# A decoder step on one core: the three gathered blocks taken through selection first, the short sequences placed beside the other five

## The chip, the core and the metric

The kernel runs on one core of a Trainium2 chip. A core has five engines that work side by side, each with its own queue in the order of the program: PE (TensorE, matmuls; PEld is its loading of weights), DVE (VectorE), ACT (ScalarE), POOL (GpSimd) and SP (SyncE). They meet by semaphores. DMAs are issued from the queues of SP, ACT and POOL. The metric is the device time of one execution in microseconds (us); lower is better.

## What is computed

One layer for 1024 prompt tokens (8 blocks of 128) and for 8 short sequences of 4 new tokens each, which attend to 2048 cached positions in pages. The reference, cut to what matters:

```python
def _layer(x, pos, h0, attend, ...):
    xn = _rmsnorm(x, norm_mix)
    z = xn @ w_in
...
    o_lat = attend(q_nope, q_rope, c_kv, k_rope, w_uk, g_kn)
    o_att = jnp.einsum('bthc,chd->bthd', o_lat, w_uv)
    y_ssm, h_last = _s5(u, h0, a_re, a_im, log_dt, b, c, d_skip)
    gl = jax.nn.gelu(y_ssm) @ w_glu
    glu = gl[..., :SSM_WIDTH] * jax.nn.sigmoid(gl[..., SSM_WIDTH:])
    x = x + jnp.concatenate([glu, o_att], axis=-1) @ w_out
    x = x + _peer(_rmsnorm(x, norm_ffn), peer_wq, peer_keys, peer_u, peer_v)

def block(xb):
    q = (xb @ wq).reshape(PEER_BLOCK, PEER_HEADS, 2, PEER_HALF)
    s = jnp.einsum('qhcd,ckd->qhck', q, keys)
    s1, i1 = lax.top_k(s[:, :, 0], PEER_TOPK)
    s2, i2 = lax.top_k(s[:, :, 1], PEER_TOPK)
    cand = (s1[..., :, None] + s2[..., None, :]).reshape(PEER_BLOCK, PEER_HEADS, kk)
    cidx = (i1[..., :, None] * PEER_KEYS + i2[..., None, :]).reshape(PEER_BLOCK, PEER_HEADS, kk)
    top, sel = lax.top_k(cand, PEER_TOPK)
    idx = jnp.take_along_axis(cidx, sel, axis=-1)
    g = jax.nn.softmax(top, axis=-1)
    act = jax.nn.gelu(jnp.einsum('qhkd,qd->qhk', jnp.take(u_tab, idx, axis=0), xb))
    return jnp.einsum('qhk,qhkd->qd', g * act, jnp.take(v_tab, idx, axis=0))
```

`attend` is causal over the prompt, and for the short sequences it goes over the cache and the new tokens. `block` is the inside of `_peer` for 128 tokens: it finds 128 of 16384 experts for each token (8 heads, 16 each) by scores against two sets of 128 keys, the best 16 of each and the best 16 of their sums, then takes a dot product with the expert's row of `peer_u` and a weighted sum of its rows of `peer_v`.

## The kernel before

The order of each engine's queue is made at build time: the Python code emits instructions in program order, a scheduler with a model of durations moves ready ones up, and tiles that share memory wait for each other. The stages, from `build`:

- Input projection, S5 and the preparation of queries and keys, to about 367 us.
- `attention` for all 8 blocks, one unit a head and block: `scores` writes `s` on PE (one buffer), DVE takes the maximum `mx`, ACT the exponent `p`, `weigh` turns `p` on PE into `pt`, DVE and ACT copy it to `pT`, PE adds `po`. `close` ends a block. The job passed to it, `split_wq`, splits the query weights of PEER into two parts and writes them to `wq_d`.
- `mix_out` for all blocks: the output projection `oz` with `w_out`, the residual and the norm; rows go to `x1_d` and `xn_d` in DRAM.
- `score` for all blocks in 16 steps (`m`): a weight tile `rw` from `wq_d` on POOL's queue, `rq` (24 matmuls a chunk), `rsc` against the keys, and `top16` on DVE for each block.
- `select`: the second top 16 and the turning of places into expert numbers, nearly all on DVE (`cand`, `top`, `sel`, `ri`, `rj`, `eq`, `kn`).

The 8 prompt blocks then go two ways. The first three (`early`, `D0 = 3`) are *gathered* by `Sparse`: for each of 128 places a row of `peer_u` and later of `peer_v` per token is fetched by an indirect DMA on POOL's queue into a ring of five rows (`RB`), and DVE does a dot product (`pu`, `pact`) or a multiply-add (`pacc`). With the short sequences that makes 832 gather steps. The other five (`late`) are *dense*: `Gates` writes a table of gates for all experts to `g_d` (`gps` on PE, `h` and `hv` on DVE), and `Dense` multiplies all of `peer_u` and `peer_v` (`da`, `dres`, `dy`), in 32 groups of four.

`Sample` is the attention of the short sequences: per sequence a `cache` gather on POOL, transposes `ltp`, splits `slh` and `sll`, products `kk`, sums of squares `ssq` on DVE, then `soften` (with the scores `sno`) and `gather`. Its `run` yields after each of 8 steps a sequence. In the code before it stands after the selection of the late blocks, but its memory is set aside early, and the scheduler moves its steps up, to beside attention.

`weave` runs `rest` (what follows the first selection) and `sparse.run` together: each yielded weight, times `PACE` 0.3, lets out gather steps of 1.5, and `behind` holds their issue behind the last DVE and PE instruction so far. In the dense stage the weight is 5.7 times `DENSE_PACE`.

## Time and profile before

| | us |
|---|---|
| median of 3 runs | 3618.16 (3617.83 to 3625.24) |
| the profiled execution | 3620.32, its span 3617.9 |
| PE busy | 3347.4 (93%) |
| DVE busy | 2716.4 (75%) |
| POOL busy | 1233.4 (34%) |
| ACT busy | 1156.2 (32%) |

A busy PE is one with a matmul in flight; two neighbours overlap, so sums of durations are above busy time, and a stretch's busy time is what counts. The granted clock is 1.0 at 2.4 GHz and 0.5 at 1.2 GHz; a value between is a mean over the stretch. Stages with different limits follow each other, so shares of the whole span say little: the rows below are by stage.

### The profile page before, as it was taken

How to read it: one execution, taken by the hardware profiler on the slowest of the kernel's cores; microseconds unless marked ns; L12 is line 12 of the kernel's file. 1: busy time of each engine (PE TensorE's matmuls, PEld its weight loads, DVE VectorE, ACT ScalarE, POOL GpSimd, SP SyncE). 2: the span in 40 equal slices, each digit the busy share in tenths (PEclk: the TensorE clock that was granted, in tenths of full speed). 3: DMA queues.
4: the chain of work that ended last, by engine and by line, in shares of the span. 5: the costliest groups of instructions: out<-in, count | busy, mean ns of one | idle time of the engine just before them, and what ended most of it. 6: DMA issues, size and time to landing. Idle time of an engine off the chain costs nothing.

```text
span 3617.9 us, 52406 instructions
## 1 busy us (share of the span) xinstructions
PE 3347.4 (93%) x19464; PEld 2929.9 (81%) x19464; DVE 2716.4 (75%) x5777; ACT 1156.2 (32%) x2268; POOL 1233.4 (34%) x1044
## 2 busy tenths in 40 slices
PE   8899899999999634998799999999999999999999
PEld 7778687765799523987798898889988989998898
DVE  7674664434577998779688888888888888888884
ACT  4333454422322422456522121222222222222221
POOL 1020100000000104222155556555555556555551
PEclk9889799999999866778899999999999999999999
DMA  3335931143322207777899999999999999999992
GB/s 132 86 88 155 315 130 46 48 152 111 115 82 71 87 26 250 290 248 252 294 308 312 318 318 325 320 315 341 321 314 313 342 333 318 326 317 324 327 328 104
DMA packets 324606, 832.19 MB, mean 230 GB/s; under 512 B 36696, under 2 KB 150488, under 8 KB 313536
## 3 DMA queue, kind: packets, MB, share of 16 engines
q0 software_dynamic: 130608, 510.98, 39.9%
q1 hardware_dynamic: 92752, 247.75, 20.0%
q10 hardware_dynamic: 100992, 70.13, 6.7%
q8 instruction: 153, 2.51, 0.3%
q14 instruction: 101, 0.83, 0.1%
HBM read 734.44 MB, written 92.94 MB: 229 GB/s over the span
## 4 chain that ended last, share of the span: by engine, by line
PE 42%; issue 19%; POOL 13%; DMA 13%; DVE 11%; ACT 2%; SPq 0%; ACTq 0%; POOLq 0%; DVEq 0%
POOL pv L1335 9%; DMA pv<-in_peer_v_dram,idx 6%; POOL pu L1335 4%; PE gps L1219 4%; PE oz L1029 3%; DMA pu<-in_peer_u_dram,idx 2%; DVE pu L1349 2%; PE po L709 2%; PE s L688 2%; PE kk L139 2%; PE rqp L139 2%; PE rqp L140 2%; PE rqp L141 2%; PE kk L141 1%; PE kk L140 1%
## 5 line engine op out<-in xcount | busy, mean ns | idle before, releaser
L1335 POOL DMA_INDIRECT pu<-in_peer_u_dram,idx x384 | 522.6, 1361 | 618.3 <-DVE pact L1349 478.9
L1335 POOL DMA_INDIRECT pv<-in_peer_v_dram,idx x384 | 521.4, 1358 | 391.2 <-DVE pacc L1361 282.9
L139 PE MATMUL da<-xdh,uh 128*128 128x320 f32 x2048 | 636.8, 311 | 19.0 <-ACT ga L1292 18.7
L141 PE MATMUL da<-xdh,ul 128*128 128x320 f32 x2048 | 634.8, 310 | 2.3 <-DVE ul L129 2.3
L140 PE MATMUL da<-xdl,uh 128*128 128x320 f32 x2048 | 635.1, 310 | 0.0
L1361 DVE SCALAR_TENSOR_TENSOR pacc<-pv,pw,pacc 128x1024 f32<-128x1024 f32 x416 | 533.8, 1283 | 100.0 <-DMA pv<-in_peer_v_dram,idx 90.8
L1349 DVE CUSTOM_DVE_ANT_0 pu<-pu,pxn 128x1024 f32<-128x1024 f32 x416 | 496.7, 1221 | 90.2 <-DMA pu<-in_peer_u_dram,idx 82.5
L139 PEld LDWEIGHTS da<-xdh,uh 128*128 128x128 f32 x2048 | 387.1, 189 | 30.3 <-ACT ga L1292 23.5
L140 PEld LDWEIGHTS da<-xdl,uh 128*128 128x128 f32 x2048 | 387.1, 189 | 6.4
L141 PEld LDWEIGHTS da<-xdh,ul 128*128 128x128 f32 x2048 | 386.6, 189 | 6.3 <-DVE ul L129 2.8
L139 PE MATMUL dy<-vh,hh 128*128 128x512 f32 x768 | 302.5, 394 | 20.4 <-DVE yac L1308 20.4
L140 PE MATMUL dy<-vl,hh 128*128 128x512 f32 x768 | 299.8, 391 | 0.0
L141 PE MATMUL dy<-vh,hl 128*128 128x512 f32 x768 | 298.0, 390 | 0.0
L128 ACT CAST uh<-ur 128x1024 fp32r<-128x1024 f32 x128 | 134.5, 1051 | 394.3 <-PE da L140 391.3
L1292 ACT ACTIVATE ga<-da 128x320 f32<-128x320 f32 x256 | 110.0, 432 | 428.6 <-PE da L141 426.8
L1219 PE MATMUL gps<-hv,h 128*128 128x128 f32 x800 | 203.8, 415 | 23.8 <-DVE hv L1212 5.5
L128 ACT CAST vh<-vr 128x1024 fp32r<-128x1024 f32 x128 | 132.0, 1049 | 249.2 <-DMA vr<-in_peer_v_dram 180.0
L129 DVE TENSOR_TENSOR vl<-vr,vh 128x1024 fp32r<-128x1024 f32 x128 | 156.4, 1223 | 60.1 <-ACT vh L128 59.6
L1219 PEld LDWEIGHTS gps<-hv,h 128*128 128x128 f32 x800 | 168.8, 242 | 39.8 <-issue 16.4
L139 PE MATMUL dres<-vh,hh 128*128 128x512 f32 x512 | 200.5, 392 | 0.0
L140 PE MATMUL dres<-vl,hh 128*128 128x512 f32 x512 | 199.6, 392 | 0.0
L139 PEld LDWEIGHTS dy<-vh,hh 128*128 128x128 f32 x768 | 144.2, 188 | 54.5 <-DVE yac L1308 25.2
(528 smaller groups left out, 7148.1 us busy)
## 6 DMA issues: line engine op xcount, KB each, us to landing
ur<-in_ut_dram SPq DMA_DIRECT2D x128, 512.0 KB, 6.3
vr<-in_peer_v_dram SPq DMA_DIRECT2D x128, 512.0 KB, 6.5
g_d<-gbuf SPq DMA_DIRECT2D x20, 2048.0 KB, 7.6
gt<-g_d ACTq DMA_DIRECT2D x32, 1280.0 KB, 18.1
wq_d<-wq POOLq DMA_DIRECT2D x16, 1024.0 KB, 7.8
rwp<-wq_d POOLq DMA_DIRECT2D x16, 1024.0 KB, 5.1
rwn<-wq_d POOLq DMA_DIRECT2D x16, 1024.0 KB, 5.4
wqr<-in_peer_wq_dram SPq DMA_DIRECT2D x16, 512.0 KB
```

The source lines that it names most:

```text
L128: nc.scalar.copy(hi, raw)
L129: nc.vector.tensor_tensor(lo, raw, hi, OP.subtract)
L139: nc.tensor.matmul(out, ah, bh, start=(first and i == 0), stop=False)
L140: nc.tensor.matmul(out, ah, bl, start=False, stop=False)
L141: nc.tensor.matmul(out, al, bh, start=False, stop=(last and i == n - 1))
L688: nc.tensor.matmul(s[:, c0 : c0 + w], qT[:, h, :], kT[:, h, c0 : c0 + w], start=True, stop=c0 + w != nk)
L1029: nc.tensor.matmul(z[:n], cat[:, k, :n], w[:, k, hs], start=(k == 0), stop=(k == 7))
L1219: nc.tensor.matmul(ps[:, :, j - j0], h1[:, j], hv[:, :, j] if j < GV else ha[:, j - GV], start=True, stop=True)
L1292: nc.scalar.activation(ga[:, cs], ps[:, :HW], AF.Gelu_apprx_tanh)
L1335: self.nc.gpsimd.indirect_dma_start(out=r, out_offset=None, in_=self.a[table], in_offset=bass.IndirectOffsetOnAxis(ap=ix, axis=0))
L1349: nc.vector.tensor_tensor_reduce(ur, ur, xn, 1.0, 0.0, OP.mult, OP.add, act[:, s : s + 1])
L1361: nc.vector.scalar_tensor_tensor(acc, vr, w[:, s : s + 1], acc, OP.mult, OP.add)
```

## The change

The early blocks alone go through `mix_out`, `score` and `select` first. `attention` becomes a generator of units for all blocks that the caller steps: 24 units (with `split_wq`, in its own pool, beside 16 of them), then the early stages. The units of blocks 3 to 7 come from `rest`: `beside` steps `smp.run` once a unit after the first 20 of them (`ATT_FREE`), twice a block of `mix_out`, once a step of `score`, and three times a block after each part of the late selection. `score`, `mix_out` and `ranks` are called once more, and `wq_d` and `w_out` are read once more. `Sample` now takes its memory after the first selection; the ring of the gathers takes it before attention. The weights yielded in those stages and in the gates, and `DENSE_PACE` (2.35 to 2.16), are new. The diff, cut to its core:

```diff
     sparse = Sparse(nc, tc, a, hold, x1_d, xn_d)
-    es = ExitStack()
-    with right():
-        smp = Sample(es, nc, tc, a, ident, keep, o_d)
+    sparse.open(ctx.enter_context(tc.tile_pool(name="ring", bufs=1)))
     wq_d = dram.tile([16, 128, 2, 8, 128], F32R, name="wq_d")
...
-    drive(attention(nc, tc, a, ident, qkv, o_d, early + late, lambda pool: split_wq(nc, a, pool, wq_d)))
-    drive(mix_out(nc, tc, a, gl_d, o_d, x1_d, xn_d, early + late, "e"))
-    xd = ctx.enter_context(tc.tile_pool(name="xd", bufs=1))
-    xt = tuple(xd.tile([128, 8, TD], F32R, name=nm) for nm in ("xdh", "xdl"))
-    et = ExitStack()
+
+    att = attention(nc, tc, a, ident, qkv, o_d, early + late)
+    next(att)
+    with right(), tc.tile_pool(name="wqs", bufs=2) as pool:
+        for _, _ in zip(split_wq(nc, a, pool, wq_d), range(16)):
+            next(att)
+    for _ in range(8 * D0 - 17):
+        next(att)
+    drive(mix_out(nc, tc, a, gl_d, o_d, x1_d, xn_d, early, "e", "right"))
+    with right(), ExitStack() as e1:
+        tv, ti = tops(e1, D0, "e")
+        drive(score(nc, tc, a, ident, xn_d, [(early, None)], lambda b: tv[:, b], lambda b: ti[:, b], "e", wq_d, 2, "right"))
+        pools = ranks(e1, nc, tc, a, "e")
+        for b0, n in SSEL:
+            select(nc, pools, early[b0 : b0 + n], tv[:, b0 : b0 + n], ti[:, b0 : b0 + n], sparse.take)
+    es = ExitStack()
     with right():
-        tv, ti = tops(et, NB, "p")
-    drive(score(nc, tc, a, ident, xn_d, [(early, None), (late, xt)], lambda b: tv[:, b], lambda b: ti[:, b], "p", wq_d))
-    sparse.open(ctx.enter_context(tc.tile_pool(name="ring", bufs=1)))
-    er = ExitStack()
-    slots = er.enter_context(tc.tile_pool(name="slots", bufs=1))
-    i1T, wT = (slots.tile([128, TD], F32, name=nm) for nm in ("i1T", "wT"))
-    i2T = slots.tile([128, TD], BF16, name="i2T")
-
-    def take_dense(b, i1, i2, w, pool, pp):
+        smp = Sample(es, nc, tc, a, ident, keep, o_d)
+
+    def take_dense(dst3, b, i1, i2, w, pool, pp):
         cs = slice((b - D0) * 128, (b - D0) * 128 + 128)
         tp = pp.tile([128, 3, 128], F32, name=f"slt{b}", tag="slt")
-        for j, (src, dst) in enumerate(((i1, i1T), (i2, i2T), (w, wT))):
+        for j, (src, dst) in enumerate(zip((i1, i2, w), dst3)):
             nc.tensor.transpose(tp[:, j], src, ident)
             nc.scalar.copy(dst[:, cs], tp[:, j])
 
-    e2 = ExitStack()
-    pools = ranks(e2, nc, tc, a, "p")
-    for b0, n in SSEL:
-        select(nc, pools, early[b0 : b0 + n], tv[:, b0 : b0 + n], ti[:, b0 : b0 + n], sparse.take)
-
     def rest():
 
-        for b0, n in DSEL:
-            bs = slice(D0 + b0, D0 + b0 + n)
-            select(nc, pools, late[b0 : b0 + n], tv[:, bs], ti[:, bs], take_dense)
-            yield 25.0 * n
-        e2.close()
+        short_att = smp.run()
+
+        def beside(steps, n, first=0):
+
+            for i, _ in enumerate(steps):
+                if i >= first:
+                    for _ in range(n):
+                        next(short_att, None)
+                    yield
+
+        for _ in beside(att, 1, ATT_FREE):
+            yield 15.0
+        for _ in beside(mix_out(nc, tc, a, gl_d, o_d, x1_d, xn_d, late, "d"), 2):
+            yield 40.0
+        xd = ctx.enter_context(tc.tile_pool(name="xd", bufs=1))
+        xt = tuple(xd.tile([128, 8, TD], F32R, name=nm) for nm in ("xdh", "xdl"))
+        et = ExitStack()
+        with right():
+            tv, ti = tops(et, ND, "d")
+        for _ in beside(score(nc, tc, a, ident, xn_d, [(late, xt)], lambda b: tv[:, b - D0], lambda b: ti[:, b - D0], "d", wq_d), 1):
+            yield 5.0
+        er = ExitStack()
+        slots = er.enter_context(tc.tile_pool(name="slots", bufs=1))
+        i1T, wT = (slots.tile([128, TD], F32, name=nm) for nm in ("i1T", "wT"))
+        i2T = slots.tile([128, TD], BF16, name="i2T")
+        dst3 = i1T, i2T, wT
+        with ExitStack() as e2:
+            pools = ranks(e2, nc, tc, a, "d")
+            for b0, n in DSEL:
+                bs = slice(b0, b0 + n)
+                select(nc, pools, late[b0 : b0 + n], tv[:, bs], ti[:, bs], lambda *x: take_dense(dst3, *x))
+                for _ in range(3 * n):
+                    next(short_att, None)
         et.close()
-        drive(smp.run())
+        drive(short_att)
         es.close()
...
             yield w * 0.5
             for _ in range(GATES_AT_ONCE):
                 if next(gates, 1) is None:
-                    yield GT * 0.5
+                    yield 1.5
         for _ in gates:
-            yield GT * 0.5
+            yield 1.5
...
 GATES_AT_ONCE = 2
 PACE = 0.3
-DENSE_PACE = 2.35
+DENSE_PACE = 2.16
+ATT_FREE = 20
...
-def attention(nc, tc, a, ident, qkv, o_d, blocks, job, side="left"):
+def attention(nc, tc, a, ident, qkv, o_d, blocks, side="left"):
...
-        extra = job(sp)
         fetch(blocks[0])
...
-            if b >= 2:
-                next(extra, None)
             yield 0.5 + 0.55 * (b + 1)
```

The order that comes out, at three places. DVE in the selection. Before, the third gathered block: `top`, `sel`, `re`, `ge` and the like are selection, `sol` and `olat` are steps of a short sequence.

```order
L1186 MAX top_8946<-cand_8936 128x8
L1187 MAX_INDEX sel_8947<-top_8946,cand_8936 128x8
L940 TENSOR_SCALAR sol_12987<-spo_12966,srs_12861 128x256
L1187 MAX_INDEX sel_8947<-top_8946,cand_8936 128x8 x5
L1141 TENSOR_TENSOR re_8988<-top_8946 128x128
L1150 CAST sf_8995<-sel_8947 128x128
L944 COPY olat<-spl_12989 128x16x4
L1151 TENSOR_SCALAR ov_8998<-sf_8995 128x128
L1156 TENSOR_SCALAR ge_8999<-sf_8995 128x128
L1144 TENSOR_REDUCE rsm_8991<-re_8988 128x8
```

The same engine after, in the first gathered block's selection (`eq`, `kn`, `fi`, `idx`), with `mx`, `pT` and `rsum` of attention's blocks 6 and 7:

```order
L731 COPY pT_5_7871<-pt_5_0_7872 128x512
L1193 TENSOR_TENSOR eq_1_0_6225<-eq_1_0_6225,kf_1_0_6223 128x2048
L718 TENSOR_REDUCE mx_7_7950<-s_7_7946 128x1
L1195 TENSOR_TENSOR eq_1_0_6225<-eq_1_0_6225 128x8x128
L1195 TENSOR_TENSOR eq_1_0_6225<-eq_1_0_6225 128x8x64
L1195 TENSOR_TENSOR eq_1_0_6225<-eq_1_0_6225 128x8x32
L1197 TENSOR_TENSOR kn_6222<-eq_1_0_6225 128x128
L1353 SCALAR_TENSOR_TENSOR fi_6232<-kn_6212,kn_6222 128x128
L731 COPY pT_6_7954<-pt_6_4_7961 128x384
L1354 CAST idx<-fi_6232 128x128
L740 RECIPROCAL rsum_7279<-rsum_7279 128x8
```

What stands between selection steps there is attention, where it was the short sequences.

DVE in the scores. Before, `tvp`, `tip` and `rssp` of the top 16 follow each other:

```order
L1185 MATCH_REPLACE rssp_2_0_7070<-tvp,rssp_2_0_7070 128x128 x4
L1186 MAX tvp<-rssp_2_0_7070 128x8 x4
L1187 MAX_INDEX tip<-tvp,rssp_2_0_7070 128x8 x2
L1183 MAX tvp<-rssp_2_4_7097 128x8
L1187 MAX_INDEX tip<-tvp,rssp_2_0_7070 128x8 x2
L1184 MAX_INDEX tip<-tvp,rssp_2_4_7097 128x8
L1185 MATCH_REPLACE rssp_2_4_7097<-tvp,rssp_2_4_7097 128x128
L1186 MAX tvp<-rssp_2_4_7097 128x8
L1187 MAX_INDEX tip<-tvp,rssp_2_4_7097 128x8
```

After, in the scores of the late blocks, with `ssq` and `sll` of a short sequence and gather steps (`pu`, `pact`):

```order
L1210 MAX tvd<-rssd_3_4_10608 128x8
L1211 MAX_INDEX tid<-tvd,rssd_3_4_10608 128x8
L904 TENSOR_REDUCE ssq_8059<-ssqr_9_9064 128x8
L129 TENSOR_TENSOR sll_6_9106<-ltp_6_9100,slh_6_9105 128x512
L904 TENSOR_REDUCE ssq_8059<-ssqr_10_9109 128x8
L129 TENSOR_TENSOR sll_7_9224<-ltp_7_9218,slh_7_9223 128x512
L904 TENSOR_REDUCE ssq_8059<-ssqr_11_9128 128x8
L1373 ISA pu_61_9147,pact_7100<-pu_61_9147,pxn_7098 128x1024
L1373 ISA pact_7100 128x1
L1373 ISA pu_62_9150,pact_7100<-pu_62_9150,pxn_7098 128x1024
```

Gathers and short sequences moved in between the steps of the top 16; before, the gathers began in the late selection.

PE in attention. Before, block 3 beside the first short sequence (`ltp`, `kk`):

```order
L861 MATMUL ltp_0_9919<-ident,cache_0_9907 128x128 x4
L861 MATMUL ltp_1_9930<-ident,cache_0_9907 128x128 x4
L709 MATMUL po_4831<-pT_5_4949,va 64x128 x3
L702 MATMUL pt_6_0_4972<-ident,p_6_4947 128x128 x3
L139 MATMUL kk_0_0_9940<-sukh,slh_0_9924 128x256
L140 MATMUL kk_0_0_9940<-sukl,slh_0_9924 128x256
L139 MATMUL kk_0_1_9948<-movh,slh_0_9924 128x288
L140 MATMUL kk_0_1_9948<-movl,slh_0_9924 128x288
L688 MATMUL s_0_4991<-kT,uqT_4798 128x512
L689 LDWEIGHTS identb
L689 MATMUL s_0_4991<-cmask,identb 128x128
```

After, block 5 beside the scores of the early blocks (`rqe`, `rsce`):

```order
L140 MATMUL rqe_1_0_5361<-rxle_5259,rwe_5358 128x384
L1115 MATMUL rsce_0_0_5337<-keyse,rqTe_0_5310 128x128 x3
L141 MATMUL rqe_1_0_5361<-rxhe_5258,rwe_5358 128x384
L736 MATMUL po_6844<-pT_2_6903,va 64x128 x3
L729 MATMUL pt_3_0_6929<-ident,p_3_6901 128x128 x4
L715 MATMUL s_5_6945<-kT,uqT_6602 128x512
L715 MATMUL s_5_6945<-kT,uqT_6602 128x256
L716 LDWEIGHTS identb
L716 MATMUL s_5_6945<-cmask,identb 128x128
L139 MATMUL rqe_2_0_5411<-rxhe_5258,rwe_5408 128x384
L140 MATMUL rqe_2_0_5411<-rxle_5259,rwe_5408 128x384
```

The short sequences left attention, and the early scores stand there instead; `kk` now comes after attention's last unit.

## Rows read from the trace of the kernel before

**Rows 1.** Windows by stage: from:to, length, busy by engine, clock, DMA share, GB/s.

```profile
367.00:455.00 88.00, 74.60 (x370) 52.88 (x369) 52.39 (x125) 42.08 (x100) 11.83 (x18) 0.81 0.95 315
455.00:776.00 321.00, 311.98 (x2210) 249.36 (x2209) 165.40 (x297) 150.57 (x399) 13.33 (x24) 0.99 0.24 85
776.00:970.00 194.00, 188.34 (x881) 118.04 (x881) 81.38 (x223) 53.63 (x147) 5.36 (x9) 0.99 0.40 131
970.00:1180.00 210.00, 209.85 (x1432) 209.24 (x1432) 153.91 (x991) 43.04 (x97) 7.99 (x15) 1.00 0.21 71
1180.00:1300.00 120.00, 74.58 (x531) 64.84 (x531) 113.16 (x614) 49.62 (x123) 11.39 (x15) 0.83 0.19 66
1300.00:1429.00 129.00, 36.71 (x161) 16.79 (x161) 122.27 (x464) 29.05 (x43) 43.13 (x29) 0.58 0.49 166
1429.00:1500.00 71.00, 70.73 (x371) 66.85 (x372) 48.93 (x65) 32.33 (x71) 16.77 (x18) 0.70 0.72 260
1500.00:1630.00 130.00, 127.16 (x702) 117.35 (x700) 97.72 (x134) 67.66 (x146) 31.84 (x32) 0.80 0.74 262
1630.00:1783.00 153.00, 133.62 (x674) 124.60 (x672) 143.41 (x277) 97.82 (x201) 38.55 (x31) 0.85 0.74 269
1783.00:3618.00 1835.00, 1789.56 (x9940) 1621.65 (x9940) 1497.48 (x1770) 444.27 (x642) 1011.31 (x747) 0.99 0.90 311
```

**Rows 2.** Waits of PE, 1180 to 1429 us: in total, times, longest.

```profile
PE srp L894 <- DVE sno L889: 51.6, 2, 41.6
```

**Rows 3.** DMA issues on the page: times, KB each, us to landing.

```profile
rwp<-wq_d POOLq DMA_DIRECT2D x16, 1024.0 KB, 5.1
```

**Rows 4.** DVE by line, 1180 to 1429 us: times, busy us, mean ns.

```profile
L1349 DVE CUSTOM_DVE_ANT_0 pu<-pu,pxn 128x1024 f32<-128x1024 f32 x28 | 32.9, 1212 | 0.8 <-DMA pu<-in_peer_u_dram,idx 0.8
...
L880 DVE TENSOR_REDUCE ssq<-ssqr 128x8 f32<-128x512 f32 x28 | 18.9, 673 | 0.6 <-ACT ssqr L877 0.6
...
L129 DVE TENSOR_TENSOR sll<-ltp,slh 128x512 fp32r<-128x512 f32 x14 | 9.5, 680 | 3.2 <-ACT slh L128 3.2
```

**Rows 5.** Windows of the instructions on kk, ltp, spo and rqp alone.

```profile
420.00:1360.00 940.00, 238.32 (x1536) 205.17 (x1536) 0.00 (x0) 106.84 (x384) 0.93 0.28 95
...
420.00:1360.00 940.00, 41.39 (x256) 31.64 (x256) 43.88 (x64) 37.24 (x64) 0.93 0.28 95
...
420.00:1360.00 940.00, 27.03 (x280) 10.71 (x280) 5.15 (x16) 0.93 0.28 95
...
960.00:1180.00 220.00, 193.88 (x1152) 178.26 (x1152) 21.30 (x48) 1.00 0.22 73
```

**Rows 6.** DVE by line, 455 to 970 us.

```profile
L880 DVE TENSOR_REDUCE ssq<-ssqr 128x8 f32<-128x512 f32 x100 | 68.2, 682 | 46.7 <-ACT ssqr L877 45.4
...
L129 DVE TENSOR_TENSOR sll<-ltp,slh 128x512 fp32r<-128x512 f32 x48 | 33.0, 690 | 27.1 <-ACT slh L128 26.0 <-PE kk L141 0.8
```

**Rows 7.** Window in attention before the short sequences begin.

```profile
405.00:418.50 13.50, 12.00 (x63) 6.95 (x61) 7.10 (x14) 5.69 (x15) 2.03 (x4) 0.95 0.91 320
```

**Rows 8.** DVE, then PE, by line and shape, 690 to 755 us.

```profile
L691 DVE TENSOR_REDUCE mx<-s 128x1 f32<-128x1024 f32 x5 | 6.1, 1225 | 5.1 <-PE s L689 5.1
...
L704 DVE COPY pT<-pt 128x512 f32<-128x512 f32 x8 | 5.5, 688 | 6.2 <-PE pt L702 6.2
...
L709 PE MATMUL po<-pT,va 128*64 128x128 f32 x128 | 17.2, 279 | 0.0
L702 PE MATMUL pt<-ident,p 128*128 128x128 f32 x64 | 10.2, 281 | 0.1
L688 PE MATMUL s<-kT,uqT 96*128 96x512 f32 x20 | 9.5, 598 | 0.0
```

**Rows 9.** Tile cache: duration ns min/median/max, first and last start us, forms.

```profile
L861 PE MATMUL ltp<-ident,cache x256: 270/273/476, 450.5 to 1275.3; 128*128 128x128 f32 x128
...
L827 POOL DMA_INDIRECT cache<-in_cache_dram,pidx x16: 940/972/1028, 434.1 to 1258.3; - x16
```

**Rows 10.** The page's first line.

```profile
span 3617.9 us, 52406 instructions
```

## The prediction

> **What bounds the kernel now.** I read the stages first [rows 1]: lengths against PE's busy time, then DVE's, then the clock. From 367 us to 1180 (attention, projection, scores) PE is the bound: idle 13.4 us in 367 to 455, 9.0 in 455 to 776, 5.7 in 776 to 970, 0.2 in 970 to 1180. From 1180 to 1429 it is not: PE is busy 74.6 of 120 and 36.7 of 129 us, DVE 113.2 and 122.3. That is the selection, of the gathered blocks and then of the others, and PE has 137.7 idle us there; PE's largest wait is for DVE's `sno` [rows 2], a step of the short sequences that stands behind selection work. From 1429 to 1783 the gates run with 22.5 us of idle PE, at a granted clock of 0.70 to 0.85 of 2.4 GHz, so part of the time at 1.2. From 1783 to the end the dense stage has PE busy 1789.6 of 1835 us. So between 367 and 1783 PE is idle 188.4 us, three quarters of it in the selection, and the dense stage behind can give little.
>
> **What the change does, and the sum.** The program does the same matmuls, so the sum is made of PE's idle time and clock between 367 us and the end of the gates. It adds a second reading of `wq_d` and `w_out` (16 and 8 transfers): the DMA share there is 0.21 to 0.40 after 455 us [rows 1], so I cost them at nothing; if that cover failed, 16 loads at 5.1 us [rows 3] would be 82 us, which is a rival below.
>
> Prices first. Selection: DVE was busy 235.4 us in 1180 to 1429 [rows 1]; 32.9 of that are gather steps, 28.4 are `ssq` and `sll` of the short sequences [rows 4], and some 10 small steps of those, an estimate; 164 remain for 8 blocks, 21 us a block, 63 for the three gathered blocks and 105 for the five others. A gather step: 1.2 us on DVE [rows 4], 1.3 with the read of its sum, an estimate. One short sequence: on PE 238.3 + 41.4 + 27.0 over 8 [rows 5], 38, and about 40 with its small products; on DVE 16 `ssq` at 0.68 and 8 `sll` at 0.69 [rows 6] and about 5 of small steps, 21 us. The orders of the two programs give the counts: 145 gather steps stand ahead of the dense stage instead of 93, 27 of them in the gates instead of 65, about 63 in the scores of the late blocks and 14 in their selection.
>
> Stretch by stretch, the idle time of PE that I expect:
>
> *Up to 455 us*: as before, 13.4.
>
> *Blocks 3 and 4 without the short sequences*, which now come later. The nearest row is a stretch of attention before they begin: PE busy 12.0 of 13.5 us [rows 7], 11% idle. Over some 105 us that is 12. Bounds 5 (the projection of the early blocks stands in the gaps) and 25 (a wait for each copy of a longer block). Taken: 12, by that row.
>
> *Block 5 beside the early scores*: the scores had next to no idle PE [rows 1]; 5, bounds 0 and 12.
>
> *Blocks 6 and 7 beside the first selection.* One head of block 7 costs PE 2.15 (`po`) + 1.28 (`pt`) + 1.9 (`s`), about 5.4 us [rows 8], and DVE 1.2 (`mx`) and half the time a 0.69 copy. By the order 15 heads stand there: PE 8 x 5.4 + 7 x 4.7 = 76; DVE 28, and 63 of selection, 91. So DVE sets this stretch, at 91, 15 over PE. Attention's `mx` and `pT` now stand behind selection steps in DVE's queue, and PE waits for them; 5 more. Taken: 20, bounds 13 and 40.
>
> *The short sequences begin* only when the first selection has given back its memory. Before, 16 us lay between their first cache gather and the first transpose [rows 9]. One head and the close of block 7 cover some 6. Taken: 10, bounds 4 and 16.
>
> *Projection of the late blocks beside two short sequences*: 776 to 970 was such a stretch, with 5.7 idle [rows 1]. Taken: 6, bounds 3 and 12.
>
> *Late scores.* PE: 121, five eighths of the 193.9 of `rqp` [rows 5], some 10 of `rscp`, and two short sequences, 80: 211. DVE: five eighths of the 153.9 of 970 to 1180 [rows 1], 96; 63 gathers, 82; two sequences, 42: 220. DVE sets it, by 9; for two queues that wait for each other I add 14. Taken: 23, bounds 9 and 40.
>
> *Late selection beside the other four short sequences.* DVE: 105 + 84 + 14 gathers at 1.3, 18: 207. PE: 160. The difference is 47, a little less by the tail of the sequences, where the selection is over and PE is the bound. Taken: 42, bounds 25 and 75 (a wait as long as the one for `sno` again).
>
> *Gates*: 38 gathers fewer are 49 us less on DVE, which was busy 143.4 of 153 us in 1630 to 1783 [rows 1]. Idle was 22.5; taken: 12, bounds 5 and 22.
>
> That is 13 + 12 + 5 + 20 + 10 + 6 + 23 + 42 + 12 = 143 us of idle PE where there were 188: 45 us less.
>
> *Clock.* In 1180 to 1429 PE ran at 0.83 and 0.58 [rows 1]: 74.6 x 0.17 + 36.7 x 0.42 = 28 us at most come back if the same work runs beside enough other matmuls to stay at 2.4 GHz. Taken: half, 14; bounds 0 and 28. In the gates the clock is a matter of its own: 1500 to 1630 has PE busy 127.2 of 130 us and a clock of 0.80. A stretch in which PE hardly rests still gets the lower level part of the time, so I count nothing there. The Trainium skill (TensorE: Matmul & The Clock Gate, Part 1: The HAM clock gate) says that the lower clock is the default and that activity releases it; by that, gates that follow a busy stretch would come out at the full clock, and the sum would be some 66 us lower. The trace does not agree in that stretch of 0.80, and the measurement decides.
>
> *Dense stage.* 52 gather steps fewer, 68 us less DVE in a stage where DVE is busy 1497.5 of 1835 and PE idle 45 [rows 1]. Taken: 3, bounds 0 and 10. Its end is still PE's: the last gathers stand ahead of the last group in both orders.
>
> The sum: 45 + 14 + 3 = 62 us. The profiled execution took 3620.3 us with a span of 3617.9 [rows 10]; the median of the runs shown is 3618.2, 2 us below it, so 3618.2 - 62 = **3556 us**. With all terms at their good ends the idle time is 77, and 111 + 28 + 10 = 149 us are gained (3469); at their bad ends it is 255, and 67 are lost (3685). Terms of separate stretches don't all fall one way: 3512 to 3600 for this case.
>
> **Rivals.** *The gates at the full clock.* If the clock stayed up after the late selection, the 331.5 us of busy PE in the gates, at a mean of 0.80 [rows 1], would cost up to 66 less: 3490. For it: the gates now follow a stretch in which PE is busy about 80% of the time instead of a third. Against it: the 0.80 in 1500 to 1630.
>
> *Slower: POOL's queue holds back the late weights.* The loads of `rwd` and the copies `krc` of the short sequences stand on POOL behind gathers that wait for a row which DVE must free, and DVE is the fuller engine there (220 against 211). If DVE falls more than about two of the sixteen steps behind, 26 us, each further load starts late and PE waits for it: up to 16 x 5.1 = 82 us [rows 3], so 3556 + 82 = 3638. For it: DVE's load, and five gathers in a row in the order. Against it: the score steps can't run ahead of DVE anyway, and loads are asked for a step early.
>
> *No change.* The selection costs PE the same 17 us a block (137.7 over 8) beside attention and the sequences as it did alone, because DVE serves in order; then the idle time is 188 again and the clock drops in the same way: 3615. For it: `sno` [rows 2]. Against it: the order puts other matmuls into those stretches, for the first time.
>
> That the change doesn't do what it says is ruled out: in the order the first selection stands among attention's steps, and the first gather ahead of the late scores.
>
> **How the numbers follow.** Forecast 0.60, gates at the full clock 0.14, no change 0.08, slower 0.18. Differences under 0.2%, 7 us, are about what a measurement of this kernel can't tell from none. Faster 0.74, same 0.08, slower 0.18. The range takes in the forecast's own, most of the first rival and the third, and leaves out the worse part of the slow case: 3495 to 3622.
>
> **What would show it.** In the profile after, the gates end near 1724 us instead of 1783, and from there to the end it takes the same 1835 us within 10. The stretch of the first selection should last 90 to 110 us with PE three quarters busy; the late scores some 235 with DVE over 90%; the late selection about 205 with PE at 75 to 80%. Wrong would be: a dense stage that is shorter by tens of us, PE waits on `rwd` of tens of us, or an idle PE of 40 us and more in the attention of blocks 3 and 4.

## The result: 1.3% slower, and where the 55 us stand

The changed kernel takes 3666.7 us (median of 4 runs, 3649.9 to 3676.7), the kernel before 3621.7 in the same comparison (3617.8 to 3628.0): a ratio of 1.0128, interval 1.0100 to 1.0155. The forecast was 3556. The profiled execution took 3674.4 us, and the page says

```profile
span 3672.6 us, 52437 instructions
```

against 3617.9 [rows 10]. Windows of the changed kernel by stage; the columns are those of [rows 1]: from:to, length, busy us (instructions) of PE, PEld, DVE, ACT and POOL, PE's granted clock, DMA share, GB/s.

```profile
367.00:455.00 88.00, 72.56 (x309) 49.06 (x307) 43.08 (x107) 36.20 (x85) 4.91 (x9) 0.67 0.71 239
455.00:600.00 145.00, 122.73 (x500) 69.31 (x500) 51.30 (x99) 38.47 (x80) 6.40 (x12) 0.89 0.58 199
600.00:712.00 112.00, 112.00 (x676) 99.72 (x674) 68.03 (x381) 27.04 (x60) 7.52 (x14) 1.00 0.40 138
712.00:812.00 100.00, 74.26 (x409) 50.15 (x407) 89.33 (x414) 38.09 (x59) 6.98 (x8) 0.91 0.15 43
812.00:1010.00 198.00, 167.36 (x833) 119.29 (x834) 126.72 (x279) 53.53 (x155) 65.04 (x60) 0.90 0.76 258
1010.00:1225.00 215.00, 204.94 (x1536) 198.49 (x1534) 194.82 (x815) 66.26 (x187) 82.60 (x79) 0.98 0.65 227
1225.00:1381.00 156.00, 97.58 (x625) 81.91 (x625) 150.81 (x665) 63.60 (x153) 30.98 (x23) 0.73 0.25 78
1381.00:1519.00 138.00, 94.42 (x667) 76.72 (x667) 56.57 (x120) 42.81 (x123) 5.86 (x10) 0.77 0.21 71
1519.00:1600.00 81.00, 78.21 (x377) 64.03 (x376) 65.83 (x96) 52.20 (x109) 24.98 (x11) 0.98 0.57 211
1600.00:1740.00 140.00, 140.00 (x793) 130.73 (x791) 66.99 (x78) 60.57 (x135) 11.52 (x18) 0.73 0.58 216
1740.00:1862.00 122.00, 111.11 (x563) 101.06 (x562) 113.87 (x217) 87.27 (x179) 32.28 (x15) 0.94 0.57 210
1862.00:3673.00 1811.00, 1788.84 (x9988) 1624.18 (x9988) 1444.22 (x1686) 448.17 (x645) 949.47 (x695) 1.00 0.88 301
```

Length less PE's busy time is its idle time. The first selection stands at 712 to 812, the late projection and the begin of the short sequences at 812 to 1010, the late scores at 1010 to 1225, the late selection at 1225 to 1381. Then, from 1381 to 1519, stands a stretch that the prediction had only as a short tail: DVE is busy 57 of 138 us, PE 94, at a clock of 0.77, and only the last short sequences run. The gates run from 1519 to 1862, the dense stage after them.

From 367 us to the end of the gates PE is idle 220 us (188 before), and busy 1275 us where it was 1228, with the same matmuls. Weighing the busy time of each row by one less its clock gives 159 us here and 114 by [rows 1]; by this estimate the lower clock accounts for 45 of the 48. It is a rough one: in the gates the weighed loss falls from 67 to 46, and the busy time only from 331.5 to 329.3. The dense stage is 24 us shorter (1811 against 1835). 31 + 48 - 24 is the 55 us between the spans (the medians are 45 apart).

Why is there such a stretch? The instructions on `kk` alone, 192 matmuls (second number in brackets counts their weight loads) a sequence, in the changed kernel:

```profile
812.00:1010.00 198.00, 72.13 (x432) 61.93 (x432) 0.00 (x0) 29.60 (x108) 0.90 0.76 258
1010.00:1225.00 215.00, 58.31 (x384) 51.92 (x384) 0.00 (x0) 26.87 (x96) 0.98 0.65 227
1225.00:1381.00 156.00, 63.90 (x384) 56.98 (x384) 0.00 (x0) 26.46 (x96) 0.73 0.25 78
1381.00:1519.00 138.00, 53.99 (x336) 47.66 (x336) 0.00 (x0) 23.26 (x84) 0.77 0.21 71
```

and in the kernel before (9 more ahead of 455 us):

```profile
455.00:776.00 321.00, 126.59 (x825) 108.53 (x824) 0.00 (x0) 58.09 (x208) 0.99 0.24 85
776.00:1180.00 404.00, 57.49 (x366) 48.33 (x366) 0.00 (x0) 25.65 (x92) 0.99 0.30 100
1180.00:1429.00 249.00, 52.62 (x336) 46.87 (x336) 0.00 (x0) 22.99 (x84) 0.70 0.35 118
```

Before, 1200 of the 1536 (6.2 sequences) were done when the scores ended at 1180, and the other 1.8 lay beside the selection. After, they begin at 825 and not at 453, 816 (4.2 sequences) are done at the end of the scores, two lie beside the late selection, and 1.8 behind it, with nothing else to run. PE's waits in that last stretch are those of one chain (total, times, longest):

```profile
PE oz L1053 <- DMA cat<-gl_d: 16.2, 1, 16.2
PE srp L918 <- DVE sno L913: 12.2, 3, 6.4
```

The first is the projection of the short rows (the 32 new tokens of the eight sequences), whose loads go out at 1500 us, behind the last sequence: by the program they land in memory that `Sample` has just given back.

### The profile page after: what moved, and what is told of

Same layout as the page of the kernel before. It is cut to its first block, busy times and chain, and to the rows that moved or that the text cites. A ratio compares the mean times of both kernels' runs of the same rounds, so it can differ in the third digit from the quotient of the medians.

```text
span 3672.6 us, 52437 instructions
## 1 busy us (share of the span) xinstructions
PE 3392.7 (92%) x19464; PEld 2951.8 (80%) x19464; DVE 2713.2 (74%) x5778; ACT 1162.5 (32%) x2270; POOL 1269.6 (35%) x1060
## 4 chain that ended last, share of the span: by engine, by line
PE 51%; issue 17%; DVE 10%; DMA 10%; POOL 9%; ACT 1%; SPq 0%; ACTq 0%; POOLq 0%; DVEq 0%
POOL pv L1359 5%; PE da L139 4%; PE da L141 4%; PE da L140 4%; PE oz L1053 4%; PE gps L1243 4%; POOL pu L1359 4%; DMA pv<-in_peer_v_dram,idx 4%; PE dy L139 3%; PE dy L140 2%; PE dy L141 2%; DVE pu L1373 2%; PE dres L141 1%; PE dres L140 1%; PE dres L139 1%
## 5 line engine op out<-in xcount | busy, mean ns | idle before, releaser
L1359 POOL DMA_INDIRECT pv<-in_peer_v_dram,idx x384 | 546.8, 1424 | 562.0 <-DVE pacc L1385 457.2
L141 PE MATMUL dres<-vh,hl 128*128 128x512 f32 x512 | 186.1, 390 | 2.1 <-DVE hl L129 1.9
```

The lines of the kernel that those rows point to most:

```text
L141: nc.tensor.matmul(out, al, bh, start=False, stop=(last and i == n - 1))
L1359: self.nc.gpsimd.indirect_dma_start(out=r, out_offset=None, in_=self.a[table], in_offset=bass.IndirectOffsetOnAxis(ap=ix, axis=0))
```

## Experiments

The changed kernel was also run beside the experiments, to have a base:

> The changed kernel once more, unedited, as the base for the runs beside it: 3650 to 3685 us, gates from about 1519 us, dense stage 1810 us.

It took 3671.3 us (before: 3619.8; ratio 1.0137). From the end of attention to the gates, the gates, and, last, a stretch in attention that the clock experiment needs (the dense stage takes 1816 us):

```profile
806.00:1516.00 710.00, 569.05 (x3674) 481.29 (x3673) 530.76 (x1879) 227.55 (x621) 186.83 (x173) 0.86 0.50 173
1516.00:1858.00 342.00, 328.75 (x1726) 295.21 (x1725) 246.66 (x390) 199.53 (x421) 68.79 (x44) 0.87 0.58 212
395.00:467.00 72.00, 52.57 (x208) 32.80 (x207) 28.79 (x43) 27.30 (x59) 6.11 (x11) 0.69 0.88 305
```

### Can the sequences be placed earlier by the code's order?

```diff
-mix_out(..., late, "d"), 2):
+mix_out(..., late, "d"), 4):
-score(..., "d", wq_d), 1):
+score(..., "d", wq_d), 2):
```

> The changed kernel with four instead of two steps of the short sequences beside each block of the late projection, and two instead of one beside each step of the late scores. Theory 1 (the short sequences outlast the late selection, which ends at 1380 us, and the gates wait for them until 1519): the sequences now end with the selection or before it, the gates start 60 to 100 us earlier, near 1420 to 1460, and the run takes 3575 to 3615 us. Rival (the same work only changes places, the late projection and scores get longer by what the end gets shorter): the gates start within 20 us of 1519 and the run takes 3645 to 3680.

It took 3691.0 us (before: 3617.6; 1.0212), and the gates start at 1516, as in the base. The rival is right about the gates; the run is even a little beyond its bound. Writing steps earlier did not make them run earlier: counted from one first `kk` to the next, a sequence takes 78 to 103 us beside other work, as in the base (80 to 117), and some 57 at the end. The reading here is that a sequence goes as fast as its chain of transposes, splits, products and sums lets it; what of the 80 to 117 us is the chain and what its place in the engines' queues no run separates.

A second try tied the last three late blocks' selection behind five more sequence steps each:

> The changed kernel with the last three blocks of the late selection each tied behind five more steps of the short sequences, so that selection lies beside the last sequences. Theory 6 (the bare end of 112 us between the late selection and the end of the sequences comes of DVE's order, which takes the selection first): the sequences end 25 to 50 us earlier than 1487, the gates start between 1465 and 1490, and the run takes 3620 to 3650 us. Rival (a short sequence needs its 50 us and more one behind the other, and at the end of the scores four are left, whatever lies beside them): the gates start within 15 us of 1516 and the run within 15 us of 3671.

3673.8 us (before: 3620.3; 1.0149). The last step of each sequence on DVE, in the base and here (durations in ns: min, median, max; first and last start in us), and the late selection here:

```profile
L968 DVE COPY olat<-spl x8: 202/212/225, 957.9 to 1487.0; 128x64 f32<-128x64 f32 x8
L969 DVE COPY olat<-spl x8: 205/221/225, 952.7 to 1474.8; 128x64 f32<-128x64 f32 x8
1212.00:1467.00 255.00, 171.58 (x1205) 149.37 (x1205) 201.97 (x821) 100.58 (x264) 25.82 (x33) 0.78 0.19 64
```

The last selection now ends at 1467 instead of 1374, with sequences beside it, but the sequences end at 1475 (base 1487) and the gates start at 1501. The rival again: four sequences are left at the end of the scores, and they need their time one behind the other. With selection and sequences side by side, neither engine is full: PE is busy 172 of 255 us, DVE 202.

### What do the gathers cost that were moved ahead?

```diff
-yield 15.0   # and 40.0, 5.0
+yield 0.0
-DENSE_PACE = 2.16
+DENSE_PACE = 2.56
```

> The changed kernel without gather steps ahead of the gates (the weights of the early stretches are zero; 2.56 instead of 2.16 in the dense stage, so that they end in time). Theory 2 (the gather steps fill DVE in the late projection, scores and selection, and PE waits for DVE there): the stretch from 812 us to the start of the gates, 707 us long, gets shorter by 40 us or more. Theory 1 (only the order of sequences and selection counts): it gets shorter by less than 15. Under both the dense stage gets longer; between before and the changed kernel 52 fewer steps went with 25 us less, 0.5 us a step, so some 120 more steps are 60 us, and the run takes 3700 to 3730 under theory 1 and 3650 to 3690 under theory 2.

3678.3 us (before: 3617.6; 1.0175). End of attention to the gates, gates, dense stage:

```profile
804.00:1459.00 655.00, 543.75 (x3672) 464.09 (x3671) 404.36 (x1646) 227.87 (x621) 38.13 (x57) 0.89 0.27 94
1459.00:1796.00 337.00, 326.92 (x1776) 293.73 (x1774) 248.41 (x409) 199.21 (x422) 51.28 (x43) 0.89 0.60 222
1796.00:3668.00 1872.00, 1787.23 (x9940) 1621.40 (x9940) 1570.60 (x1899) 444.92 (x643) 1111.65 (x812) 0.98 0.92 323
```

With 2 gather steps ahead of the gates instead of 118 the first stretch is 655 us instead of 710, about 0.5 us a step; the dense stage, with 116 more, takes 1872 instead of 1816. Theory 2 holds, and its other half too: what a step ahead costs is what it gives back. That it is DVE's part of a step that PE waits for is argued: with the steps their DMAs went too (DMA share 0.27 instead of 0.50).

Two more runs on the same price. More steps in the late selection and the bare end:

> The changed kernel with gather steps let out in the late selection and in the end of the short sequences, where none are now: 25 to 45 more ahead of the gates. DVE is busy 39.8 of 96 us from 1400 to 1496. Theory 1: the gates start within 10 us of 1519, the dense stage, with 20 us of idle PE left, gains 5 to 15, and the run takes 3655 to 3670 on a comparison in which the changed kernel takes 3667. Theory 2 (each gather step on DVE is waited for by PE): the gates start 20 to 50 us later, and the run takes 3680 to 3710.

3708.9 us (before: 3617.6; 1.0259):

```profile
1520.00:1880.00 360.00, 337.10 (x1736) 296.52 (x1736) 250.43 (x384) 199.70 (x424) 76.62 (x44) 0.86 0.57 213
1880.00:3700.00 1820.00, 1790.44 (x9988) 1626.32 (x9988) 1412.60 (x1659) 447.54 (x645) 923.55 (x668) 1.00 0.85 292
```

The gates start at 1520, so the late selection and the bare stretch hide the 26 steps more that now stand there, as theory 1 says; but the gates get 18 us longer, and the dense stage gains nothing from 27 steps fewer: PE was already busy 1792 of 1816 us there. Neither theory had that; the time is in theory 2's range, though not by its way. In the gates themselves stand 28 steps instead of 27, so why they got longer stays open. And in the kernel before:

> The kernel before with the weights of the gates raised by half and 2.16 instead of 2.35 in the dense stage: about 30 to 35 gather steps more ahead of the dense stage, taken from it. Theory 2 (a gather step on DVE is waited for wherever it stands, about 0.5 us): the gates get 10 to 25 us longer, the dense stage as much shorter, and the run takes the same as before within 8 us. Rival (the 25 us that the dense stage gains in the changed kernel are there for fewer gather steps alone, and the gates have room): the gates get less than 5 us longer, the dense stage 12 to 20 shorter, and the run is 10 to 20 us faster than before.

3624.5 us (before: 3619.8; 1.0010, interval 0.9996 to 1.0025). Gates and dense stage:

```profile
1430.00:1804.00 374.00, 328.84 (x1741) 306.55 (x1742) 326.75 (x538) 198.66 (x417) 137.02 (x113) 0.80 0.81 295
1804.00:3623.00 1819.00, 1787.20 (x9945) 1623.60 (x9943) 1465.05 (x1705) 445.90 (x644) 983.20 (x715) 0.99 0.89 305
```

20 us more in the gates, which now hold 98 gather steps instead of 66, and 16 less in the dense stage [rows 1]: the same exchange.

### What does the lower clock cost?

```diff
+ for k in range(5):
+     nc.tensor.transpose(FILL[0][:, k % 4, :], p[:, 0:128], ident)
```

> The changed kernel with five extra transposes a head, into a bank of their own that nobody reads, between the scores and po of blocks 0 to 2 of attention (up to about 467 us; 395 to 512 us had a clock of 0.63 with PE busy 87 of 117 us). Theory 3 (PE fell to the lower clock there because it rests between the steps, and this costs time): the clock of 395 to 467 rises above 0.85 and block 2 ends 8 to 20 us earlier than 467. Rival (the chain of copies between the steps sets the pace at either clock): block 2 ends within 5 us of 467 or later, whatever the clock, and the run takes the same as the changed kernel within 10 us.

3676.2 us (before: 3617.6; 1.0163). 395 to 467 us:

```profile
395.00:467.00 72.00, 63.38 (x393) 44.70 (x392) 34.57 (x58) 34.01 (x81) 6.68 (x12) 0.95 0.96 324
```

The base has a clock of 0.69 at 395 to 467 (0.53 in the first profile). With the extra transposes it is 0.95, so the half of theory 3 on the clock is shown: more matmuls in the rests, and the clock rises. What this is worth in time is not. Block 2 ends (its last `po`) at 455, 12 us ahead of the 467 that the theory named, but only 3 ahead of the base, where it ends at 458. Attention's last `po` starts at 782 instead of 806, but most of those 24 us come in blocks that have no extra transposes, and the program with them also comes out in another order (block 0 ends at 410 instead of 389). And nothing of it arrives: the first `kk` starts at 823 (821), and PE stands 21 us, 784 to 805, ahead of the first product of `Sample`'s set-up. The weights of that product are asked for at 797, 10 us after the set-up's first load (2 us in the base); what held them is not settled. The gates start 11 us earlier and end at 1858 as in the base, at a clock of 0.84 instead of 0.87. Where the gates gave those 11 us back is not settled.

### What do the last sequences cost?

> The changed kernel with six of the eight short sequences; the attention of the last two is left out. Theory 4 (the short sequences run one behind the other from 820 us on, at 50 us where they run alone and 80 beside other work; the last ones are bare, and the gates wait for them): the gates start 80 to 100 us earlier than 1519, and the run is 80 to 100 us shorter. Rival (the late selection on DVE, to 1381, with what follows it, holds the gates): less than 45 us shorter, which is what the two sequences cost DVE.

3569.5 us, 102 less than the base. The stretch from the last late selection to the gates is now

```profile
1367.00:1412.00 45.00, 19.89 (x116) 10.51 (x117) 14.08 (x29) 6.05 (x13) 1.15 (x1) 0.56 0.37 126
```

45 us instead of 142. Theory 4. In the kernel before:

> The kernel before with the same two sequences left out. Theory 4 says that here the last sequences lie beside the selection, where DVE is the bound: only their DVE work comes off, 2 x 21 us, and the run is 25 to 45 us shorter than the kernel before. Rival (a sequence costs the same wherever it stands): as much shorter as the changed kernel gets without them.

3525.8 us, 94 less than the 3619.8 beside it, which theory 4 did not expect: the number is close to the rival's, 102. Selection, then gates:

```profile
1179.00:1397.00 218.00, 127.97 (x557) 100.97 (x555) 205.20 (x1006) 46.44 (x73) 56.33 (x52) 0.55 0.55 188
1397.00:1689.00 292.00, 261.63 (x1328) 240.51 (x1328) 282.01 (x450) 194.76 (x402) 81.98 (x65) 0.92 0.74 267
```

The selection is 31 us shorter, as expected; the gates are 61 shorter. With the sequences done earlier, the projection and scores of the short rows (`oz`, `rqn`), which stood in the gates, ran beside the selection, where PE is idle. So the end of the sequences has a price in both kernels: what hangs on it cannot use the idle PE.

Then could the gates fill the bare end?

```diff
+ gb = Gates(eb, ...)          # ahead of the last sequence steps
+ for _ in short_att:
+     for _ in range(3): next(gates)
```

> The changed kernel with the memory of the gates set aside before the short sequences give theirs back (one of the two 16 KB output buffers only after that), and three gate steps let out at each of the last sequence steps. Theory 4 (between the end of the late selection at 1380 us and 1519 the gates are ready and only stand behind the last two sequences, which leave PE and DVE half empty): the first gates run from about 1385 to 1400 us, the dense stage starts 50 to 90 us earlier, and the run takes 3580 to 3620 us, at or under the kernel before. Rival (gates and sequences hold each other up by as much, or the later end of the sequences only makes the stage of the short rows the last one): the dense stage starts less than 25 us earlier.

3674.4 us (before: 3617.4; 1.0159). Gates beside sequences, the end of the sequences, the rest:

```profile
1386.00:1454.00 68.00, 67.90 (x448) 62.77 (x449) 48.48 (x71) 43.56 (x108) 4.45 (x6) 0.93 0.28 112
1454.00:1570.00 116.00, 83.40 (x502) 59.89 (x500) 41.77 (x91) 32.90 (x88) 3.83 (x6) 0.78 0.23 78
1570.00:1855.00 285.00, 275.19 (x1450) 253.60 (x1448) 201.32 (x336) 162.02 (x343) 53.94 (x39) 0.83 0.61 222
```

The first gates run at 1386, as theory 4 says, and the dense stage starts at 1855 instead of 1858: the rival. The gates that ran ahead made the sequences end 39 us later (1526), and the short rows' stage and the rest of the gates behind them keep PE busy 275 of 285 us.

### The late start alone, and the rest alone

The short sequences of the kernel before, begun only behind attention:

> The kernel before with the short sequences begun only behind attention (three steps beside each block of the projection, one beside each step of the scores, three beside each late block's selection, as the changed kernel places them), everything else as before: one part of the change alone. Theory 4 (beside attention the sequences filled rests of PE that stay empty without them, and the last ones come to lie beyond the selection): attention ends 90 to 110 us earlier than 751, the gates start 25 to 60 us later than 1429, and the run takes 3640 to 3680. Rival (PE is full up to the scores' end either way, and the order of its work there is worth nothing): the gates start within 12 us of 1429, and the run takes 3610 to 3632.

3670.7 us (before: 3620.3; ratio 1.0134, interval 1.0107 to 1.0161). Attention, projection, scores, selection, gates:

```profile
455.00:635.00 180.00, 161.91 (x953) 112.03 (x952) 70.39 (x93) 66.20 (x131) 3.19 (x6) 0.97 0.21 70
635.00:885.00 250.00, 233.43 (x1222) 162.22 (x1221) 108.68 (x273) 76.58 (x218) 10.58 (x17) 0.96 0.44 147
885.00:1167.00 282.00, 282.00 (x2055) 276.82 (x2054) 203.41 (x1115) 86.48 (x227) 13.98 (x25) 1.00 0.21 70
1167.00:1459.00 292.00, 159.69 (x1003) 129.81 (x1001) 255.09 (x1105) 99.21 (x232) 50.91 (x48) 0.71 0.30 103
1459.00:1844.00 385.00, 346.07 (x1773) 312.37 (x1772) 291.27 (x487) 199.52 (x421) 120.87 (x82) 0.82 0.69 248
```

One part of the change alone costs what the whole change does. Attention ends at 635 instead of 751, but the last sequence ends at 1430 instead of 1364, the gates start at 1459, and with the short rows later in them they take 385 us instead of 353. Theory 4 holds, though attention ends 116 us earlier and not 90 to 110.

Then both kernels without the sequences:

> The kernel before with the attention of all eight short sequences left out (only its set-up and its output projection remain), as the base for the run beside it. Six of them lie where PE is full and two beside the selection: the run takes 3290 to 3350 us.

3500.8 us. 367 us to the gates, gates, dense stage:

```profile
367.00:1381.00 1014.00, 704.10 (x3621) 523.43 (x3620) 541.71 (x2431) 220.52 (x437) 73.67 (x86) 0.80 0.38 123
1381.00:1657.00 276.00, 249.38 (x1280) 227.81 (x1280) 268.61 (x365) 189.93 (x393) 81.62 (x67) 0.96 0.77 274
1657.00:3503.00 1846.00, 1791.58 (x9941) 1622.04 (x9940) 1495.65 (x1769) 444.95 (x643) 1017.99 (x747) 0.99 0.90 309
```

> The changed kernel with the same left out. Theory 7 (the first selection beside attention is a gain by itself, as the sum had it, and the late sequences alone turn it into a loss): 20 to 60 us faster than the kernel before without sequences, with at most 110 us of idle PE from 600 us to the gates. Rival (the order of the blocks gains nothing in itself, since PE waits for DVE as much beside attention as in the selection): within 15 us of the kernel before without sequences, or slower.

3402.7 us, 98 less than the kernel before without them:

```profile
367.00:1339.00 972.00, 725.29 (x3604) 542.63 (x3602) 636.39 (x2599) 215.26 (x428) 182.74 (x193) 0.81 0.58 199
1339.00:1588.00 249.00, 243.75 (x1280) 223.47 (x1280) 227.88 (x271) 192.35 (x399) 36.47 (x27) 0.98 0.59 220
1588.00:3400.00 1812.00, 1781.72 (x9940) 1619.55 (x9940) 1440.23 (x1683) 443.89 (x641) 939.90 (x695) 0.99 0.87 300
```

Theory 7, at more than it said, though with more idle PE than it said (209 us from 600 to the gates). All three stretches are shorter: 42, 27 and 34 us; the 34 stand in the dense stage, which has 51 gather steps fewer. The expectation for the kernel before missed by 150 us, and the miss is the lesson: eight sequences cost it 117 us (3617.5 - 3500.8), a little over a third of the 8 x 40 us of PE work that the prediction gave them. And 77 of the 117 are the gates (276 us instead of 353), which the short rows' scores left (`rqn` runs at 537 to 661 us here). So most of the sequences' own work stood in rests of PE: without them PE is idle 310 us from 367 to the gates, with them 166. In the changed order the eight cost 269 us (3671.3 - 3402.7).

Beside the runs with six sequences this says more. From none to six, the kernel before pays 25 us (3525.8 - 3500.8) and the changed one 167 (3569.5 - 3402.7); the last two cost 94 and 102. So the bare end is what holds the gates in the changed kernel, but it is not what sets the two kernels apart: that is the first six, which cost next to nothing where they stood before.

### Versions that beat both

One line of the kernel before moved, so that the sequences are done before the selection:

```diff
+drive(smp.run())
 drive(score(...))
...
-drive(smp.run())     # in rest, behind the late selection
```

> The kernel before with one line moved: the short sequences are written ahead of the scores instead of behind the late selection. In the run with six sequences the gates took 292 us instead of 353, because the projection and scores of the short rows then ran beside the selection. Theory 5 (what counts is that work of PE for which something else must be finished first, here the short rows', lies beside the selection, where PE idles 138 us): the scores end 60 to 80 us later than 1180, the selection takes 210 to 225 us instead of 249, the gates 290 to 300, and the run is 5 to 30 us faster than before. Rival (the sequences cost PE as much in the scores as they free later): within 5 us of before, or slower.

3601.2 us (before: 3617.4; ratio 0.9963, interval 0.9950 to 0.9976). Scores, selection, gates:

```profile
965.00:1261.00 296.00, 295.06 (x2099) 275.48 (x2099) 198.16 (x1113) 81.52 (x212) 12.43 (x23) 1.00 0.25 82
1261.00:1478.00 217.00, 112.16 (x487) 99.81 (x487) 210.85 (x1063) 48.98 (x75) 51.85 (x51) 0.52 0.52 175
1478.00:1755.00 277.00, 251.20 (x1279) 231.18 (x1280) 270.36 (x367) 190.10 (x394) 81.73 (x67) 0.94 0.77 275
```

And with the gain of the changed order on top, the first selection beside the late scores:

```diff
 drive(smp.run()); es.close()
+drive(score(..., [(early, None)], ..., "e", wq_d))
+# then the first selection; in rest: score of late, short(), late selection, gates
```

> The kernel before with the short sequences written ahead of the scores, as in the run with one line moved (3601 us), and besides with the scores in two parts: those of the gathered blocks, then their selection beside the scores of the late blocks, and the stage of the short rows written ahead of the late selection. Theory 7 (the order gains what selection it takes out of the stretch in which only DVE works, if the sequences still start in attention): the selection left alone is that of five blocks, 105 us of DVE instead of 168, the gates start 30 to 60 us earlier than 1478, and the run takes 3545 to 3585 us. Rival (PE waits for DVE in the late scores by as much as the selection gets shorter, since DVE is busy 198 of 296 us there already): within 12 us of 3601, or slower.

3579.2 us (before: 3624.0; ratio 0.9881, interval 0.9855 to 0.9907). Scores with the first selection, late selection with the short rows, gates:

```profile
950.00:1304.00 354.00, 334.48 (x2305) 311.73 (x2304) 274.71 (x1510) 108.80 (x268) 44.08 (x60) 0.95 0.45 159
1304.00:1447.00 143.00, 87.67 (x378) 77.39 (x377) 138.14 (x669) 30.45 (x49) 33.06 (x34) 0.50 0.52 177
1447.00:1740.00 293.00, 260.21 (x1330) 241.67 (x1330) 283.61 (x408) 194.20 (x403) 86.51 (x68) 0.91 0.75 271
```

PE is busy 334 of 354 us beside 275 us of DVE, and the stretch in which DVE alone counts is 143 us instead of 249 (217 with the one line moved). The run is 45 us faster than the kernel before, where the moved line alone gave 16. Part of the difference may be the other two edits, since gather steps now start beside the late scores and the short rows stand ahead of the selection. The gain of the order is there when the sequences start in attention.

## Why the prediction was wrong

**The step that failed is the one on the late selection.** It set DVE's 207 us against PE's 160 and took the larger, with a short tail of the sequences in which PE is the bound. The places were right (two sequences beside the projection, two beside the scores, and 3.75 left), and the two sums were near: PE was busy 192 us and DVE 207 from 1225 to 1519. But sums of engines bound a stretch only if each can go on while the other works, and a short sequence is a chain through PE, ACT and DVE that takes 50 us alone and 80 to 117 beside other work, one behind the other. The stretch took 294 us instead of 205, with 102 us of idle PE instead of 42 (bound 75), and its tail, 138 us, has PE busy 94. The runs without two sequences, with selection tied behind them, and with the late start alone show this. The numbers to see it were there: [rows 5] give 38 us of PE a sequence and [rows 9] that the eight took from 450 to 1275.

**The clock** was counted as a gain of 14 (0 to 28) and is a loss of 45 by the weighing above, about as large a miss as that of the late selection (59 and 60 us); that the 45 us lie on the path is estimated and not shown. In [rows 1] the idle time was in one place, and the stretches from 455 us to it ran at 0.99 to 1.00. The change spread it: 0.67 and 0.89 in the attention of the first blocks, 0.90 in the late projection, 0.73 and 0.77 later. The prediction asked what the selection would get back and not what the other stretches, which lost their filling, would lose.

The other terms of idle PE: to 455 us 15.4 (taken 13.4); blocks 3 and 4 with the early projection 22.3 (12, inside its bounds of 5 to 25); early scores 0.0 (5); blocks 6 and 7 beside the first selection 25.7 of 100 us (20; 90 to 110 long, three quarters busy: right); begin of the sequences and late projection 30.6 (10 + 6, bounds 7 to 28 together, so just outside); late scores 10.1 in 215 us (23 in 235; DVE 91%: right); gates 13.7 (12). Without the late selection's term and the clock the idle time would have been forecast within 17 us.

**The dense stage** gave back 24 us, not 3 (bounds 0 to 10), which the prediction had named as a sign of being wrong. The prediction looked at its idle PE, 45, and took 3 of it; with 51 gather steps fewer it is 22. By the run without gather steps in front they cost about as much there, so this was no gain of the whole; the sum had charged them in front as time of DVE alone.

**The rivals.** The late weights never held PE up: no wait for `rwd` is among PE's waits in the late scores, so the slower case that was priced is not the one that came. The gates at the full clock came in part only: 0.98 at 1519 to 1600, but 0.73 at 1600 to 1740, with PE busy all 140 us, and the gates took 343 us where they had taken 354. The Trainium skill (TensorE: Matmul & The Clock Gate, Part 1: The HAM clock gate) has activity release the clock; this row, where matmuls are in flight all the time, does not agree, if busy time is taken for activity. "No change" had the selection cost PE as much beside other work as alone; it does not, since 84 us of idle PE remain in the two selections of 138, but the bare end took the difference.

A gain of the order itself, which the forecast put at 62 us, is there where the sequences are not in the way: 98 without them, 34 of it in the dense stage, and in the last version 22 to 29 beside the run with one line moved (by the medians, or by what each gained on the kernel before). Its size in the changed kernel no run shows.

## What to carry to other kernels

Before work is moved out of a stretch, ask what it filled there: work that stands in rests costs a fraction of its length, and moved to where nothing else runs it costs all of it. A chain through several engines is priced by its latency and by how many are left at a given time, not by its share of each engine; the stages that hang on its end count too. Work moved from one stretch in which an engine is nearly full to another one of that kind comes back at the same price.

## What the runs showed of the hardware

- With 115 transposes added to the first blocks of attention PE's granted clock was 0.95 instead of 0.69 in 395 to 467 us. The same kernel without them had 0.53 and 0.69 there in two executions.
- The granted clock was 0.73 in a stretch in which PE had matmuls in flight 140 of 140 us (the short rows' scores, `rqn`, among the gates), and 0.98 in the 81 us ahead of it, with gates and the projection of the short rows. In the run with one line moved, whose gates have no `rqn` in them, it was 0.94. But `rqn` alone isn't the reason: in the kernel before it was 0.83 at 1640 to 1720 us, behind the last `rqn`, with PE busy 69 of 80 us.
- A gather step, 1.2 us on DVE [rows 4], was worth about 0.5 us of the whole ahead of the gates (116 steps, 55 us), in them (32 steps, 20 us) and in the dense stage (116 steps, 56 us). It was worth nothing more in the dense stage when that had some 25 us of idle PE left, and 26 steps beside the last sequences put off the gates by under 5 us.
